# A mixture-of-experts encoder layer: who clears the gather buffers, unsized first gathers, pair sums in the last stage, and one guard around an unused position

## The chip, the cores and the metric

One core of one Trainium2 chip runs the whole layer in one launch. The metric is the device time of that core in microseconds; the profile adds one execution of the same program, with its span and every engine's instructions.

## The reference

One encoder layer over 1024 tokens of width 1024: a mixer (neighbourhood attention, a bidirectional RWKV-7 scan, pooling), then a hierarchical mixture of experts, each followed by a residual sum and a layer norm. The change touches the second half alone:

```python
u2 = layer_norm(x) * (1.0 + sc2) + sh2
# top-1 of 4 groups, then top-2 of its 8 experts; gate = pg_sel * softmax(top two logits)
hb = silu(u2[tok] @ w_gate[e]) * (u2[tok] @ w_up[e])      # 1024 -> 512
y[tok, j] = hb @ w_down[e]                                # 512 -> 1024, j = 0, 1
f = gate[:, 0] * y[:, 0] + gate[:, 1] * y[:, 1]
x = layer_norm(ALPHA * x + g2 * f) * ln2_gain + ln2_bias
```

All of it is in float32; a float32 matmul leaves two records of TensorE in the trace.

## The kernel before

After the mixer, `router` sorts the 2048 (token, choice) pairs into positions, each of one expert with up to 128, 64 or 32 rows. `route` builds on VectorE, GpSimd and ScalarE the table `idx` (which token's row goes to which partition of which position; 0 to 1023 is a row, anything above is skipped by the gather) and `code` (size and expert of each position, read by every engine as a register). Sixteen comparisons on GpSimd (L1267), each followed by a scaling on ScalarE (L1268), feed sixteen matmuls (L1323) whose result becomes `idx` (L1356). Meanwhile GpSimd clears the four row buffers `xg` with one memset (L1275), placed behind its last comparison. A barrier ends the router.

`experts` is written by hand, one program for each engine, with semaphores. There are 50 possible positions; the first 16 are always used, and from there each is under a condition on `code`. SyncE streams three 2 MB weight parts for each position through three buffers, waiting for the position's turn to be freed (the first three positions' weights are loaded before). GpSimd gathers the rows of the first four positions, later one more whenever a buffer is free; each gather reads the size of its position and picks one of three forms (32, 64 or 128 rows). `pipeline` gives the order on TensorE, ScalarE and VectorE: in step g, `head(g)` (gate and up products on TensorE, L1713 and L1721), `rows(g + 1)` (transposes of the next rows, L1692), `down(g - 1)` (L1747, L1758; on VectorE the scaling by g2 out of PSUM, L1781 and L1786), `turn(g)` (transposes of h, L1728). `by_size` is a nest of branches (L1512, L1514, L1516) around the code for 32, 128 and 64 rows; `if_used` (L1524) is one branch. On TensorE the step of the first unused position has nothing to do but `down` of the position before it: it passes over `head` by the branches of `by_size`, over `rows` and `turn` by one `if_used` each. GpSimd scatters each position's result rows to `ys_s` in DRAM, row 2 * token + j.

The last stage is written by `tail_plan` as three lists of operations. Eight 1 MB loads (L1595) bring `ys_s` back, tile tt with 128 tokens, token t on partition t with both choices beside each other. TensorE sums the two choices by two products with diagonal matrices of the gates `dg` (L1866), in two halves of 512 columns; tiles 2 and 5 also add ALPHA * x by a third product with `alpha`. For the other six VectorE adds ALPHA * x and takes the sum of the row out of PSUM (`sums`, L1878), for tiles 2 and 5 ScalarE does (L1875). Then, for each tile: VectorE the mean (L1883), ScalarE square with sum and root (L1895, L1897), VectorE two small operations (L1887, L1888), ScalarE the normalisation (L1901), VectorE gain and bias (L1891, L1892), SyncE the 512 KB store (L1639). The wait of an operation names the ones that it needs; each list runs in its order.

Of the kernel before, what the change touches and what calls it, by code (L numbers as in the profile page):

```python
# [13 lines left out]
OP = mybir.AluOpType  # L14
# [109 lines left out]
class Builder:  # L124
# [1082 lines left out]
    def route(self, p, ps):  # L1207
# [66 lines left out]
        with self.rtc.issue_after(last.ins):  # L1274
            nc.gpsimd.memset(self.xg, 0.0)  # L1275
# [185 lines left out]
    def experts(self):  # L1461
# [9 lines left out]

        gain, bias = self.late[:, 0], self.late[:, 1]
# [15 lines left out]
        names += [f"l{i}" for i in range(8)] + ["x1a", "x1b", "tail_pe", "tail_act", "tail_dve"]  # L1488
# [50 lines left out]
        def pipeline(e, rows, head, down, turn):  # L1539


            def step(g, old, c):
                new = size(e, g + 1) if g + 1 < NP else None
                head(g, c)
                if new is not None:
                    rows(g + 1, new)
                if g and down:
                    by_size(e, old, lambda t: down(g - 1, t))
                if turn:
                    turn(g, c)  # L1550
                if g + 1 == NP:
                    if down:
                        by_size(e, c, lambda t: down(g, t))
                elif down:
                    if_used(e, c, g, lambda: step(g + 1, c, new))
                else:
                    if_used(e, new, g + 1, lambda: step(g + 1, c, new))
# [9 lines left out]
        tail = self.tail_plan(sem, yall, x1a, of, ls, gain, bias, [(pgu[0], pgu[1]), tuple(pT), tuple(py)], junk)  # L1567
        with nc.Block() as blk:
            @blk.sync
            def _(e):  # L1570
# [9 lines left out]
                def finish(g):  # L1580
# [13 lines left out]
                    for tt in range(8):  # L1594
                        e.dma_start(yall[tt], self.ys_d[256 * tt:256 * tt + 256, :].rearrange("(t j) n -> t j n", j=2)  # L1595
# [39 lines left out]
                e.dma_start(g2, self.rows_d[3]).then_inc(sem("g2"), 16)  # L1635
                step(0, None)
# [6 lines left out]
            def _(e):  # L1643
# [38 lines left out]
            def _(e):  # L1682
# [41 lines left out]
                def turn(g, c):  # L1724
# [6 lines left out]
                    def both():  # L1731
                        e.wait_ge(sem("h"), g + 1)
                        with e.If(c > 1):
                            part((2, 3))
                        part((0, 1)).then_inc(sem("ht"), 1)
                    if_used(e, c, g, both)
# [96 lines left out]


# [8 lines left out]
    def tail_plan(self, sem, yall, x1a, of, ls, gain, bias, banks, junk):  # L1843
# [8 lines left out]
        dg, eps = self.late[:, 2:4].rearrange("p a (j n) -> p (a j) n", n=128), self.leps  # L1852
        gates = self.gtw.rearrange("p j t -> p (j t)")
        ident, alpha = self.C["ident"], self.C["alpha"]
# [3 lines left out]
        inside = lambda tt: tt in (2, 5)  # L1858
        pf = lambda tt: banks[tt % 3]

        def product(tt):
            def f(e):
                n = 3 if inside(tt) else 2
                for h in range(2):
                    for j in range(n):
                        i = e.matmul(pf(tt)[h], dg[:, tt + 8 * j] if j < 2 else alpha,  # L1866
                                     (yall[tt][:, j] if j < 2 else x1a[tt])[:, hs[h]], start=j == 0, stop=j == n - 1)
                return i
            free = [("sum1", tt - 3)] if tt > 2 else []
            op("pe", "mm", tt, [("dg0", tt), ("dg1", tt), (f"l{tt}", 16), ("x1" + "ab"[tt // 4], 16)] + free, f)  # L1870
# [38 lines left out]
        for tt in range(8):  # L1909
            product(tt)  # L1910
# [98 lines left out]
```

## Time and profile before

| | us |
|---|---|
| time, median of 3 runs | 1575.91 (1575.29 to 1577.81) |
| the profiled execution's own time | 1565.44 |
| its span, first to last instruction | 1563.6 |
| TensorE busy in the span | 1367.4 (87%) |
| VectorE busy | 778.7 (50%) |
| ScalarE busy | 571.8 (37%) |
| GpSimd busy | 380.4 (24%) |

The shares are averages over the mixer (to about 922 us), the router (to 947 us), the experts (to 1511 us) and the last stage, which have different limits. The profiled execution lies 10.47 us under the median of the timed runs; 1.84 us of its time lie around the span.

### The profile page before, as it was taken

To read this page: it belongs to the slowest core of one execution; us is meant where nothing else is said; L and a number is where in the kernel's file an instruction comes from. 1 tells how busy PE (TensorE), PEld (TensorE's weight loads), DVE (VectorE), ACT (ScalarE), POOL (GpSimd) and SP (SyncE) were. 2 spreads that over 40 slices of the span, in tenths; PEclk is the share of its full clock that TensorE was granted. 3 is DMA by queue.
4 is the path that set the end of the run, shared out by engine and by line. 5 is a ranking of instruction groups with operands and counts; after the bars stand their busy time and mean duration, and the time that the engine had idled before them with its cause. 6 is when DMAs were issued, how large, how long until landed. Compare 5 with 4: busy or idle time off the path is not lost. (4 is left out here: it accounts for less than half of the span.)

```text
span 1563.6 us, 24661 instructions
## 1 busy us (share of the span) xinstructions
PE 1367.4 (87%) x8190; PEld 923.9 (59%) x8190; DVE 778.7 (50%) x2002; ACT 571.8 (37%) x1182; POOL 380.4 (24%) x442
## 2 busy tenths in 40 slices
PE   5989999988869899999899745999999999899856
PEld 5778778766546677677788643444444444444422
DVE  6775886855883566565667972111111121211117
ACT  5663433414575667676544430000001000100006
POOL 3331232351337313700403331011101101111000
PEclk8999999996868899989999857999999999999968
DMA  9868899866422325315564475898878987998764
GB/s 259 223 200 303 284 318 327 298 211 186 145 64 69 93 72 150 88 35 150 187 262 162 167 275 208 338 351 324 330 291 341 380 324 306 362 369 349 262 248 193
DMA packets 163373, 371.49 MB, mean 238 GB/s; under 512 B 22880, under 2 KB 99009, under 8 KB 154227
## 3 DMA queue, kind: packets, MB, share of 16 engines
q1 hardware_dynamic: 155555, 350.59, 63.2%
q0 software_dynamic: 7632, 18.51, 3.7%
q8 instruction: 106, 1.74, 0.4%
q14 instruction: 80, 0.66, 0.1%
HBM read 365.47 MB, written 65.44 MB: 276 GB/s over the span
## 5 line engine op out<-in xcount | busy, mean ns | idle before, releaser
L1713 PE MATMUL m_pgu<-w,m_xT 128*128 128x512 f32 x448 | 197.0, 598 | 7.4 <-issue 7.2
L1713 PEld LDWEIGHTS m_pgu<-w,m_xT 128*128 128x128 f32 x448 | 84.7, 192 | 110.4 <-issue 110.3
L1656 POOL DMA_INDIRECT ys_s<-m_y,m_idx x37 | 35.0, 946 | 467.4 <-DVE m_y L1786 266.5
L197 PE MATMUL pg<-ul,w_h 128*128 128x512 f32 x320 | 128.2, 401 | 0.2 <-DVE ul L295 0.2
L196 PE MATMUL pg<-uh,w_h 128*128 128x512 f32 x320 | 126.7, 402 | 1.4 <-ACT uh L294 0.7
L198 PE MATMUL pg<-uh,w_l 128*128 128x512 f32 x320 | 126.8, 396 | 0.0
L1721 PE MATMUL m_pgu<-w,m_xT 128*32 128x256 f32 (+1 forms) x1312 | 108.0, 420 | 8.7 <-issue 8.3
L1747 PE MATMUL m_py<-w,m_hT 128*128 128x512 f32 x224 | 98.7, 594 | 9.6 <-issue 9.6
L1825 DVE TENSOR_TENSOR m_h<-m_sil,m_pgu 128x512 f32<-128x512 f32 x14 | 9.6, 688 | 192.4 <-PE m_pgu L1713 192.4
L1721 PEld LDWEIGHTS m_pgu<-w,m_xT 128*32 128x32 f32 (+1 forms) x1312 | 53.6, 116 | 54.5 <-issue 34.2
L210 DVE SCALAR_TENSOR_TENSOR acc<-wm,sc_c,acc 128x256 f32<-128x256 f32 x112 | 62.3, 557 | 27.8 <-DMA wm<-in_w_mod_dram 18.9
L1747 PEld LDWEIGHTS m_py<-w,m_hT 128*128 128x128 f32 x224 | 41.5, 190 | 57.1 <-issue 57.1
L1828 DVE TENSOR_TENSOR m_h<-m_sil,m_pgu 64x256 f32<-64x256 f32 (+1 forms) x23 | 10.8, 471 | 121.0 <-ACT m_sil L1796 121.0
L196 PEld LDWEIGHTS pg<-uh,w_h 128*128 128x128 f32 x320 | 60.6, 191 | 15.3 <-ACT uh L294 1.6
L197 PEld LDWEIGHTS pg<-ul,w_h 128*128 128x128 f32 x320 | 61.0, 191 | 14.1 <-issue 0.7
L198 PEld LDWEIGHTS pg<-uh,w_l 128*128 128x128 f32 x320 | 61.1, 191 | 13.3 <-issue 0.7
L945 DVE SCALAR_TENSOR_TENSOR sn<-s,fc,sf 64x64 f32<-64x64 f32 x168 | 47.5, 283 | 41.7 <-PE s L936 38.6
L756 PE MATMUL g<-zi,bk 64*128 64x128 f32 x384 | 54.2, 320 | 15.2 <-DMA bk<-bkd 9.3
L1758 PE MATMUL m_py<-w,m_hT 128*32 128x256 f32 (+1 forms) x656 | 56.6, 418 | 12.2 <-issue 12.2
L1781 DVE TENSOR_TENSOR m_y<-m_py,m_g 128x512 f32<-128x512 f32 x28 | 19.4, 692 | 88.0 <-PE m_py L1747 88.0
L756 PEld LDWEIGHTS g<-zi,bk 64*128 64x128 f32 x384 | 46.6, 219 | 28.0 <-issue 10.6
L1786 DVE TENSOR_TENSOR m_y<-m_py,m_g 32x256 f32<-32x256 f32 (+1 forms) x82 | 37.0, 451 | 52.3 <-PE m_py L1758 51.1
(523 smaller groups left out, 3017.8 us busy)
## 6 DMA issues: line engine op xcount, KB each, us to landing
w<-in_moe_w_gate_dram SPq DMA_DIRECT2D x37, 2048.0 KB, 8.4
w<-in_moe_w_up_dram SPq DMA_DIRECT2D x37, 2048.0 KB, 12.9
w<-in_moe_w_down_dram SPq DMA_DIRECT2D x37, 2048.0 KB, 15.9
wm<-in_w_mod_dram SPq DMA_DIRECT2D x128, 128.0 KB, 4.6
w<-in_w_in_dram SPq DMA_DIRECT2D x21, 512.0 KB, 6.7
hd<-h SPq DMA_DIRECT2D x18, 512.0 KB, 4.5
wm<-in_w_mod_dram SPq DMA_DIRECT2D x16, 512.0 KB, 6.3
w<-ys_s SPq DMA_DIRECT2D x8, 1024.0 KB, 13.0
```

The lines of the kernel that those rows point to most:

```text
L196: mm(out, lh[0], rh[0], start=start, stop=False)
L197: mm(out, lh[0], rh[1], start=False, stop=False)
L198: mm(out, lh[1], rh[0], start=False, stop=stop)
L210: nc.vector.scalar_tensor_tensor(acc, wm, self.sc_c[:, k:k + 1], acc, op0=OP.mult, op1=OP.add)
L756: nc.tensor.matmul(pa[h][:, j], bk[hs, j], zr[hs, j], start=True, stop=True)
L945: nc.vector.scalar_tensor_tensor(sn[H[h], H[h]], p[H[h], 2, H[h]], fc[H[h]], sf[H[h], H[h]], op0=OP.mult, op1=OP.add)
L1656: e.indirect_dma_start(out=self.ys_d, out_offset=off(idx[0:t, NP + g:NP + g + 1]), in_=y[0:t, g % NY], in_offset=None, bounds_check=2 * S ...
L1713: i = mm(pgu[q], xT[:, k], w[:, k], start=k == 0, stop=k == 7)
L1721: i = mm(pgu[0][o:o + t, 0:n], xT[:, k, 0:t], w[:, k, c:c + n], start=k == 0, stop=k == 7)
L1747: i = mm(py[nh], hT[:, 128 * f:128 * f + 128], wd[b][:, f, 512 * nh:512 * nh + 512], start=f == 0, stop=f == 3)
L1758: i = mm(py[0][o:o + t, 0:n], hT[:, 64 * j + t * a:64 * j + t * a + t], wd[b][:, f, c:c + n], start=f == 0, stop=f == 3)
L1786: i = e.tensor_mul(y[0:t, g % NY, c], py[0][t * j:t * j + t, 0:n], g2[0:t, c])
```

## The change

Five things change. (1) In `route` ScalarE clears `xg` (Copy of one constant column, broadcast, with scale 0), behind its own last scaling; GpSimd's memset goes. (2) In `experts` GpSimd's first four gathers take all 128 indices, without reading the size; the sizes are read after the fourth. (3) In the last stage each tile's `ys_s` rows are loaded so that a row and its pair lie on neighbouring partitions (two blocks of 128 rows); one product with a 128 x 64 matrix sums the pairs of a block (`pair` scaled by `rowg`, the gates in that order), and the two blocks fill partitions 0 to 63 and 64 to 127 of the bank. (4) There, tiles 0 to 6 get ALPHA * x by a product with `alpha` in front of (`residual`), and ScalarE takes them out of PSUM; VectorE keeps the sums of tile 7, and joins the normalisation and gain, and the root and bias, into two operations for each tile (`xm`, `add`), so that `rs`, `xn` and `gain` go. (5) In `pipeline`, for the engines that have `down` (TensorE and VectorE), one `if_used` stands around `head` and `rows`, and one around `turn` and the next step. Four small DMAs on SyncE's queue, behind that of `g2`, arrange `rowg`.

```diff
-            last = nc.gpsimd.tensor_scalar(ohr[:, j], C["iota128"], row[:, j:j + 1], None, op0=OP.is_equal)
-            nc.scalar.activation(ohs[:, j], ohr[:, j], AF.Copy, scale=C["orow1"][:, j:j + 1])
+            nc.gpsimd.tensor_scalar(ohr[:, j], C["iota128"], row[:, j:j + 1], None, op0=OP.is_equal)
+            last = nc.scalar.activation(ohs[:, j], ohr[:, j], AF.Copy, scale=C["orow1"][:, j:j + 1])
...
         with self.rtc.issue_after(last.ins):
-            nc.gpsimd.memset(self.xg, 0.0)
+            nc.scalar.activation(self.xg, C["iota128"][:, 0:1, None].to_broadcast([128, NX, D]), AF.Copy, scale=0.0)
...
             def step(g, old, c):
                 new = size(e, g + 1) if g + 1 < NP else None
-                head(g, c)
-                if new is not None:
-                    rows(g + 1, new)
-                if g and down:
-                    by_size(e, old, lambda t: down(g - 1, t))
-                if turn:
-                    turn(g, c)
...
+                def first():
+                    head(g, c)
+                    if new is not None:
+                        rows(g + 1, new)
+
+                def rest():
+                    if turn:
+                        turn(g, c)
...
+                else:
+                    if_used(e, c, g, first)
+                    if g:
+                        by_size(e, old, lambda t: down(g - 1, t))
+                    if_used(e, c, g, rest)
...
-                        e.dma_start(yall[tt], self.ys_d[256 * tt:256 * tt + 256, :].rearrange("(t j) n -> t j n", j=2)
+                        e.dma_start(yall[tt], self.ys_d[256 * tt:256 * tt + 256, :].rearrange("(s p) n -> p s n", s=2)
...
+                for s in range(2):
+                    for j in range(2):
+                        e.dma_start(rowg[j:128:2, s, :], self.gtw[64 * s:64 * s + 64, j, :]).then_inc(sem("rowg"), 16)
...
                 for g in range(NX):
+
+                    e.indirect_dma_start(
+                        out=xg[:, g], out_offset=None, in_=self.u2d, in_offset=off(idx[:, g:g + 1]),
+                        bounds_check=S - 1, oob_is_err=False).then_inc(sem(f"xg{g}"), 16)
+                for g in range(NX):
                     c.append(size(e, g))
-                    gather(g, c[g])
...
+                e.tensor_add(pair, ident[:, 0:128:2], ident[:, 1:128:2]).then_inc(sem("pair"), 1)
...
-        inside = lambda tt: tt in (2, 5)
+        inside = lambda tt: tt < 7
...
+        def residual(tt):
+            def f(e):
+                for h in range(2):
+                    i = e.matmul(pf(tt)[h], alpha, x1a[tt][:, hs[h]], start=True, stop=False)
+                return i
+            op("pe", "x1", tt, [("x1" + "ab"[tt // 4], 16)] + [(f"sum{h}", tt - 3) for h in range(2) if tt > 2], f)
...
+            def half(e, h):
+                for s in range(2):
+                    i = e.matmul(pf(tt)[h][64 * s:64 * s + 64, :], dg[:, 2 * tt + s], yall[tt][:, s, hs[h]],
+                                 start=not inside(tt), stop=True)
...
+        def centre(tt):
+            op("dve", "xm", tt, [("mean", tt), ("mm1", tt), ("late", 32)], lambda e: e.scalar_tensor_tensor(
+                xm(tt), of[tt], col(tt, 12), gain, op0=OP.add, op1=OP.mult))
+
+        def normal(tt):
             op("dve", "rec", tt, [("sd", tt)], lambda e: e.reciprocal(col(tt, 15), col(tt, 14)))
-            op("dve", "rs", tt, [("rec", tt)], lambda e: e.tensor_mul(col(tt, 16), col(tt, 12), col(tt, 15)))
...
+            op("dve", "add", tt, [("rec", tt), ("xm", tt), ("sq", tt)], lambda e: e.scalar_tensor_tensor(
+                of[tt], xm(tt), col(tt, 15), bias, op0=OP.mult, op1=OP.add))
...
-        def normal(tt):
-            op("act", "xn", tt, [("rs", tt)], lambda e: e.activation(of[tt], of[tt], AF.Identity, bias=col(tt, 16),
-                                                                    scale=col(tt, 15)))
...
+        for tt in range(2):
+            residual(tt)
         for tt in range(8):
+            if tt > 1 and inside(tt):
+                residual(tt)
             product(tt)
-        for tt in range(10):
-            if 0 < tt < 9:
-                rstd(tt - 1)
+        for tt in range(9):
             if tt < 8:
                 if not inside(tt):
                     sums(tt)
                 mean(tt)
-            if tt > 1:
-                affine(tt - 2)
-        for tt in range(9):
-            if tt < 8 and inside(tt):
-                sums(tt)
+                centre(tt)
             if tt:
                 normal(tt - 1)
-            if tt < 8:
-                deviation(tt)
+        for tt in range(8):
+            if inside(tt):
+                sums(tt)
+            deviation(tt)
```

## Rows read from the trace of the kernel before

**Rows 1.** The chain that ended last, end of experts and last stage: start, us, what.

```profile
1498.76 6.54 PE m_py L1758 x15
...
1510.88 5.23 DMA w<-ys_s
...
1516.35 6.32 PE m_pgu L1866 x8
...
1559.35 1.23 DVE w L1892
```

**Rows 2.** Busy time of the engines in stretches of 4 us, last stage.

```profile
1508.00:1512.00 4.00, 0.00 (x0) 0.00 (x0) 1.66 (x8) 0.00 (x0) 0.51 (x1) 0.50 0.39 76
...
1520.00:1524.00 4.00, 4.00 (x9) 1.76 (x8) 1.29 (x4) 0.00 (x0) 0.00 (x0) 0.79 1.01 424
...
1552.00:1556.00 4.00, 0.00 (x0) 0.00 (x0) 3.90 (x10) 2.65 (x5) 0.00 (x0) 0.55 0.33 131
```

**Rows 3.** Timeline of the router near 936 us: start, us, engine, line.

```profile
935.98 3.50 POOL L1275 MEMSET m_xg<- 128x4096 f32 x1
936.00 3.58 DVE L1312 TENSOR_SCALAR rt<-rt 128x16 int32<-128x16 int32 x1
936.06 0.40 ACT L1268 ACTIVATE rt<-rt,cst 128x128 fp32r<-128x128 f32 x1 [0.17 <-POOL rt L1267]
...
939.59 0.18 DVE L1342 TENSOR_SCALAR m_code<-m_code 1x50 int32<-1x50 int32 x1
...
946.66 0.19 DVE L1356 CAST m_idx<-rt 128x50 int32<-128x50 f32 x1
```

**Rows 4.** Groups of instructions by line and form, ScalarE and VectorE.

```profile
L1875 ACT ACTIVATE w<-m_py 128x512 f32<-128x512 f32 x4 | 2.3, 592 | 1.3 <-PE m_py L1866 1.3
...
L1895 ACT ACTIVATE w<-w,m_ls 128x1024 f32<-128x1024 f32 x8 | 9.2, 1146 | 25.9 <-DVE m_ls L1883 25.9
...
L417 DVE SCALAR_TENSOR_TENSOR t<-t,rows 128x1024 f32<-128x1024 f32 x6 | 7.3, 1218 | 0.0
...
L1878 DVE SCALAR_TENSOR_TENSOR w<-w,m_pgu 128x512 f32<-128x512 f32 x6 | 3.9, 684 | 12.8 <-PE m_pgu L1866 12.8
```

**Rows 5.** The chain that ended last, start of the experts.

```profile
947.63 0.52 POOLq L1499
...
948.53 0.04 POOLq L1648
...
949.40 2.44 DMA m_xg<-u_s,m_idx
```

**Rows 6.** Timeline: SyncE's first load of an expert's weights.

```profile
960.40 0.36 SPq L1577 DMA_DIRECT2D w<-in_moe_w_gate_dram  x1
```

**Rows 7.** DMA issues, start of the experts: KB each, median us to landing.

```profile
m_g<-rows_s SPq DMA_DIRECT2D x1, 512.0 KB, 3.4
```

**Rows 8.** Timeline, TensorE at full clock: 16 matmul records 64 and 128 wide.

```profile
1002.32 3.65 PE L1758 MATMUL m_py<-w,m_hT 128*64 128x512 f32 x16
...
1264.14 7.03 PE L1747 MATMUL m_py<-w,m_hT 128*128 128x512 f32 x16
```

**Rows 9.** Timeline of the last stage, one tile on ScalarE and VectorE.

```profile
1543.31 0.60 ACT L1875 ACTIVATE w<-m_py 128x512 f32<-128x512 f32 x1 [0.58 <-PE m_py L1866]
...
1544.61 0.21 DVE L1883 TENSOR_SCALAR m_ls<-m_ls 128x1 f32<-128x1 f32 x1 [0.82 <-ACT w L1875]
...
1545.60 1.14 ACT L1895 ACTIVATE w<-w,m_ls 128x1024 f32<-128x1024 f32 x1
...
1546.86 0.29 ACT L1897 ACTIVATE m_ls<-m_ls,m_le 128x1 f32<-128x1 f32 x1
```

**Rows 10.** TensorE's branches (PEldq), by line: ns min/median/max, first and last start.

```profile
L1512 PEldq COMPARE_BRANCH  x1: 440/440/440, 1491.3 to 1491.3; - x1
...
L1512 PEldq COMPARE_BRANCH  x1: 5522/5522/5522, 1492.4 to 1492.4; - x1
...
L1524 PEldq COMPARE_BRANCH  x67: 65/65/3813, 1179.0 to 1499.1; - x67
```

More of the change, by code (lines that the diff above doesn't have):

```diff
@@ L1470, in experts @@
         ls = sb("m_ls", [128, 8, 20])
+        pair = sb("m_pair", [128, 64])
+        rowg = sb("m_rowg", [128, 2, 8])
         gain, bias = self.late[:, 0], self.late[:, 1]
@@ L1487, in experts @@
         names = ["T0", "T1", "xT", "gu0", "gu1", "sil", "h", "h0", "ht", "hs", "y0", "y1", "e0", "e1", "late", "g2", "o"]
-        names += [f"l{i}" for i in range(8)] + ["x1a", "x1b", "tail_pe", "tail_act", "tail_dve"]
+        names += [f"l{i}" for i in range(8)] + ["x1a", "x1b", "pair", "rowg", "tail_pe", "tail_act", "tail_dve"]
         names += [f"{w}{b}" for w in "GUD" for b in range(NB)]
@@ L1543, in step @@
                 new = size(e, g + 1) if g + 1 < NP else None
-                head(g, c)
-                if new is not None:
-                    rows(g + 1, new)
-                if g and down:
-                    by_size(e, old, lambda t: down(g - 1, t))
-                if turn:
-                    turn(g, c)
[L1551 to L1555, printed above, removed]
-                else:
-                    if_used(e, new, g + 1, lambda: step(g + 1, c, new))
+                def first():
[5 more added lines that the diff above has]
+                        turn(g, c)
+                    if g + 1 == NP:
+                        if down:
+                            by_size(e, c, lambda t: down(g, t))
+                    elif down:
+                        step(g + 1, c, new)
+                    else:
+                        if_used(e, new, g + 1, lambda: step(g + 1, c, new))
+                if not down:
+                    first()
+                    rest()
+                else:
+                    if_used(e, c, g, first)
+                    if g:
+                        by_size(e, old, lambda t: down(g - 1, t))
+                    if_used(e, c, g, rest)
             c = size(e, 0)
@@ L1565, in wait @@
                 e.wait_ge(sem(name), v)
-        tail = self.tail_plan(sem, yall, x1a, of, ls, gain, bias, [(pgu[0], pgu[1]), tuple(pT), tuple(py)], junk)
+        tail = self.tail_plan(sem, yall, x1a, of, ls, gain, bias, pair, rowg, [(pgu[0], pgu[1]), tuple(pT), tuple(py)], junk)
         with nc.Block() as blk:
@@ L1729, in part @@
                         return i
[L1731 to L1736, printed above, removed]
+                    e.wait_ge(sem("h"), g + 1)
+                    with e.If(c > 1):
+                        part((2, 3))
+                    part((0, 1)).then_inc(sem("ht"), 1)
                 def down(g, t):
@@ L1840, in experts, with tail_plan @@
         ctx.close()
-    def tail_plan(self, sem, yall, x1a, of, ls, gain, bias, banks, junk):
+    def tail_plan(self, sem, yall, x1a, of, ls, gain, bias, pair, rowg, banks, junk):
         lists = {"pe": [], "act": [], "dve": []}
```

32 lines of the change are left out of this document (12 added, 20 removed).

## The prediction

> **What bounds the kernel now.** I read the page first, then the chain that ended last, then stretches of 4 us, and only then single rows; a share of the whole span says little, since each stage has its own limit. Three places of the chain are touched. In the router VectorE's chain of small operations builds `idx`, and nothing else can start before it. The experts are a long run of TensorE, started by the first gather and fed by weight loads whose first one waits for the first position; so what the start gains, the whole stage gains. The last stage starts when the loads of `ys_s` land: TensorE starts at 1516.35 and the last VectorE operation ends at 1560.58, 44.23 us later [rows 1]. In it two limits follow each other. At first TensorE is slow: the clock is 0.50 before it starts and 0.79 on average from 1520 to 1524, and its first eight records take 6.32 us [rows 1, 2]. Later VectorE is the limit: 3.90 of 4 us busy from 1552 to 1556, when TensorE has long finished [rows 2]. The loads are not: 8.4 MB at 424 GB/s leave one tile every 2.5 us [rows 2].
>
> **The change part by part.** The sum is made against the profiled execution's own 1565.44 us; the same microseconds are then taken from the median of 1575.91, since all of them lie in stages that both executions run.
>
> *Clearing the buffers.* GpSimd's memset runs from 935.98 for 3.50 us. VectorE's operation that starts at 936.00 takes 3.58 us, on 16 columns, and ends with the memset; the next one starts at 939.59 and takes 0.18 us [rows 3]. Without the memset that operation should end near 936.2, so `idx` is complete 3.4 us earlier, at 943.45 instead of 946.85. The clearing goes to ScalarE behind its last scaling, which ends at 936.46 [rows 3]. From 592 ns for 512 columns and 1146 ns for 1024 [rows 4] one column costs 1.08 ns, and 4096 of them 4.5 us: it ends at 941.0, 2.5 us ahead of the router's new end, which is its cover; nothing of ScalarE's is queued behind it in the router. At twice that length it would end at 945.5 and cost 2.1 us. Bounds of this part: 0 (if something else held VectorE) to 3.6; I take 3.4.
>
> *First gathers.* GpSimd begins to read the first size at 947.63 and reaches the first gather at 948.53; the gather starts at 949.40 and its rows are there 2.44 us after [rows 5]. Without the reading the 0.90 us go. Three things could take some of it back: the 512 KB load of `g2`, which is under way until 3.4 us after its issue [rows 7], four small DMAs queued behind it, and gathers of 128 indices in place of 32, whose surplus is skipped. If the rows come only after the load of `g2` (951.1) and four issues of 0.36 us behind it, they come 0.7 us later than the present 951.84. Bounds: -0.7 to 0.9; I take 0.6, since the rows follow the load of `g2` already now. The four DMAs also stand ahead of SyncE's weight loads, but the first of these is issued at 960.40 [rows 6], some 12 us after SyncE starts; the four need 1.5 us of them.
>
> Both gains move the first position, hence the first load and everything behind it.
>
> *The last stage.* Sixteen records of 64-wide products take 3.65 us, because two halves of the array work side by side; sixteen 128-wide ones take 7.03 [rows 8]. A tile's new product is eight 64-wide records, 1.83 us; its residual is four 128-wide ones, 1.76. The residuals of tiles 0 and 1 run right behind the last `down`, which ends at 1505.3 [rows 1], and are over before the loads land; but TensorE is then idle again for some 7 us, and I let it start slow, as before. Counting from its start at 0: full clock from 5.3 on (1521.65, between the stretch at 0.50 and the end of the one at 0.79 [rows 2]); up to there 2.65 us of full-clock work are done, and tiles 0 and 1, 3.65 of it, are ready at 6.3. Then five times 1.76 + 1.83 for tiles 2 to 6: 24.2. Tile 7, without a residual: 26.1.
>
> ScalarE for each tile: from its first sum at 1543.31 to the end of VectorE's mean at 1544.82 are 1.51 us, from the square at 1545.60 to the end of the root at 1547.15 are 1.55 [rows 9]: 3.1 with the gaps, under TensorE's 3.59. VectorE for each tile: mean 0.21, two operations on 1024 columns at 1.22 [rows 4, 9], the reciprocal and gaps 0.25: 2.9, under it too. So TensorE sets the pace, and the end is a tail on VectorE, in its order: sums of tile 6 on ScalarE and its mean at 25.3, `xm` of 6 at 26.5, `add` of 5 at 27.9, two sums of tile 7 at 0.68 [rows 4] to 29.2, mean 29.4, `xm` of 7 30.6, `add` of 6 32.0, `add` of 7 33.4. Against 44.23 that is 10.8 us less; the store behind it stays. If TensorE never ran slow, tile 7 would be ready at 23.4 and the gain 13.4; if the two halves did not work side by side, it would be ready at 39.5, and with the last sums, mean, `xm` and two `add` behind it the end lies at 45.3, a loss of 1.1. I take 10.8, because the 64-wide row has the same shape of work.
>
> The Trainium skill, "TensorE: Matmul & The Clock Gate", section "Measured speedup vs the span model", speaks against full overlap: three column tiles gave 2.38 times, not 3. If two gave 1.59 times, as an estimate from that page, a product would take 2.2 us and the gain would be 8 us. The row here has 7.03 / 3.65, 1.93 times.
>
> *The guard.* For the unused position TensorE passes three branches between 1491.3 and 1492.4, the first of 0.44 us, and then waits 5.52 us in a fourth, over the 32-row code of `down`; the last `down` starts at 1498.76 [rows 1, 10]. One guard in place of the three starts that long branch some 0.7 us earlier. Where it jumps on, the long wait stays: the same code is jumped over. Used positions keep their number of branches on TensorE (the guard of `turn` and that of the step become those of `first` and `rest`), and a guard that isn't taken costs 65 ns at the median of 67 [rows 10]; VectorE gets one more in each, in time that it waits for TensorE. Bounds: -3.8, the longest of the 67, if the longer jump brings a second long wait, to 5.5 if it brings none; I take 0.4, between nothing and the 0.7.
>
> The Trainium skill, "Runtime: NRT & Kernel Launch", section "Instruction fetch mechanics", says that a taken branch whose target lies outside the two pages at hand waits for a fetch of the target page. By it one longer jump may meet that wait just as four short ones did. It is the rule behind the first of the rivals below.
>
> The sum: 3.4 + 0.6 + 10.8 + 0.4 = 15.2 us. The profiled execution would take 1550.2, the median 1560.7.
>
> **The rivals.**
> - *The guard's jump waits twice.* Its target and the branch after it each wait, 3.8 us on top: 15.2 - 0.4 - 3.8 = 11.0, 1564.9. For it: the jump is longer than any of the three. Against it: over the code of `head` the present branch takes 0.44 us.
> - *The guard's jump doesn't wait.* The gap shrinks by 5.5: 15.2 - 0.4 + 5.5 = 20.3, 1555.6. Against it: the same code still separates the two places.
> - *The start gives nothing.* VectorE was held by something that ends with the memset by chance, and the gather waits for the load of `g2`: 15.2 - 4.0 = 11.2, 1564.7. Against it: two ends within 0.1 us of each other [rows 3].
> - *The change of the last stage doesn't do what it says.* The two 64-wide halves follow each other: 15.2 - 10.8 - 1.1 = 3.3, 1572.6. Against it: the 3.65 us.
> - *Slower.* The positions that are under a condition have their code in another order, and branches that were short wait for code. At 3.8 us for one [rows 10] four of them leave nothing of the gain, five make it slower, six give 1583.5. For it: such waits of several us exist in the trace. Against it: the number of branches and the code between them are the same.
>
> **How the numbers follow.** Chances: the forecast, within 4 us, 0.56; the guard waits twice 0.10; doesn't wait 0.10; the start gives nothing 0.06; the halves don't overlap 0.05; slower 0.06; several terms small together, so that it comes out within 0.2%, 0.04; sizes beyond 20 us 0.03. The range from 1554 to 1567 takes in the forecast and the three rivals around it, 0.82. A difference under 0.2%, 3.2 us, is about what a measurement of this kernel can't tell from none. Faster: 0.56 + 0.10 + 0.10 + 0.06 + 0.05 + 0.03 = 0.90; the same 0.04; slower 0.06.
>
> **What would show it.** Clearing: VectorE's operations near 936 take 0.2 us, ScalarE's Copy ends ahead of `idx`. Gathers: the first one starts 0.9 us earlier behind the barrier. Last stage: a product of eight records in 1.8 us at full clock, TensorE's last record 26 us after its first product, VectorE's last operation 33 us after it. Guard: one branch of several us ahead of the last `down`, as before. The prediction is wrong if the gap from the load of `ys_s` to the end shrinks by less than 7 us, or if the experts' stage between the first gather and the last `down` changes by more than 4.

## The result, and the profile after

| | before | after |
|---|---|---|
| time, median of 20 runs of each | 1575.78 us (1564.68 to 1584.72) | 1564.44 us (1555.95 to 1574.90) |
| ratio, with its 95% interval | | 0.9936 [0.9918, 0.9953] |
| the profiled execution's own time, its span | 1565.44, 1563.6 us | 1559.32, 1557.1 us |

The change makes the kernel 10.1 us faster (7.4 to 12.9), where 15.2 was forecast; the forecast of 1560.7 us lies 3.7 us under the median. The spans of the two profiled executions differ by 6.5 us alone. So the stages are read one by one.

**Router.** Timeline of the kernel after, near 937 us: start, us, engine and line, in brackets the idle time before it and what ended it.

```profile
937.38 0.15 DVE L1312 TENSOR_SCALAR rt<-rt 128x16 int32<-128x16 int32 x1
...
937.50 0.18 DVE L1342 TENSOR_SCALAR m_code<-m_code 1x50 int32<-1x50 int32 x1
...
937.74 3.60 ACT L1275 ACTIVATE m_xg<-cst 128x4096 f32<-128x4096 f32 x1
...
944.58 0.19 DVE L1356 CAST m_idx<-rt 128x50 int32<-128x50 f32 x1
```

These answer to [rows 3]. L1312, which took 3.58 us beside GpSimd's memset, takes 0.15; L1342 follows 0.12 us behind its start instead of 3.59. ScalarE clears in 3.60 us and is done at 941.34, 3.4 us ahead of `idx`. From the end of GpSimd's last comparison to the end of L1356 it was 10.82 us and is 7.37.

**Start of the experts.** The chain that ended last, kernel after:

```profile
946.39 2.68 DMA m_xg<-u_s,m_idx
949.06 0.67 issue
949.74 1.99 PE m_pT L1712 x8
```

and SyncE's two lines in the timeline there:

```profile
945.58 0.33 SPq L1648 DMA_DIRECT2D m_g<-rows_s  x1
...
945.95 2.42 SPq L1651 DMA_DIRECT2D m_rowg<-m_gt  x4
```

The load of `g2` is SyncE's first instruction behind the barrier. The gather starts 0.81 us behind it, where it was 1.74 (947.66 to 949.40). But TensorE takes its rows up 3.35 us after the gather's start, not 2.49 (0.67 of them lie behind the landing that the profile gives here; two more traces of this kernel have 3.17 and 3.52 us for the landing itself and 0.04 behind it). From the load of `g2` to TensorE it was 4.23 us and is 4.16: what the reading of the size cost is nearly all paid again, behind the gather's start.

**The unused position.** TensorE's branches by line, kernel after (ns min/median/max, start):

```profile
L1515 PEldq COMPARE_BRANCH  x1: 5748/5748/5748, 1497.0 to 1497.0; - x1
```

One long wait is left, as in [rows 10], 0.2 us longer. The guard in front of it takes 0.44 us (439 ns), and the long branch starts 2.74 us after the last gate and up product, where it was 3.40. From that product to the last `down`: 9.78 us before, 9.30 after.

**Last stage.** The chain, kernel after:

```profile
1514.64 5.35 DMA w<-ys_s
...
1520.12 3.68 PE m_pgu L1890 x8
1523.81 1.82 PE m_pT L1890 x8
1525.63 1.91 PE m_py L1883 x4
1527.55 1.87 PE m_py L1890 x8
...
1542.67 1.89 PE m_pgu L1890 x8
1544.59 0.70 ACT w L1900 x2
1545.63 1.28 DVE w L1915
...
1548.34 1.32 DVE w L1903 x4
...
1552.79 1.28 DVE w L1920
```

The stretches that answer to [rows 2] (busy us of PE, PEld, DVE, ACT, POOL with the number of instructions; PE's granted clock; DMA share; GB/s):

```profile
1520.00:1524.00 4.00, 3.88 (x10) 1.40 (x12) 0.00 (x0) 0.84 (x3) 0.00 (x0) 0.51 1.03 421
1552.00:1556.00 4.00, 0.00 (x0) 0.00 (x0) 2.04 (x3) 0.00 (x0) 0.00 (x0) 0.50 0.61 242
```

The first product (L1890, both halves of a tile) takes 3.68 us while the clock is granted at 0.51; from the second on a product takes 1.82 to 1.89 and a residual (L1883) 1.91. From 1523.81 to 1544.56 TensorE is the chain; behind ScalarE's sum of tile 6 it is VectorE, with `xm` and `add` of the last tiles and the two sums of tile 7. From the first product's start to the end of VectorE's last operation: 33.95 us (1520.12 to 1554.07), where it was 44.23 [rows 1].

**The experts between.** Busy time in the stretch from TensorE's first transpose to the last gate and up product, one row for each of four executions: the kernel before as shown,

```profile
951.89:1488.98 537.09, 500.74 (x3000) 249.54 (x3004) 89.49 (x177) 46.86 (x109) 67.24 (x70) 0.98 0.86 330
```

the kernel before in a second execution (below),

```profile
952.80:1500.15 547.35, 508.94 (x3000) 249.93 (x3004) 89.67 (x177) 46.96 (x109) 67.31 (x70) 0.97 0.84 324
```

the kernel after as shown,

```profile
949.74:1494.31 544.57, 506.56 (x3000) 248.64 (x3004) 89.41 (x177) 46.88 (x109) 66.73 (x70) 0.97 0.84 326
```

and the kernel after in a third execution (below).

```profile
946.52:1494.53 548.01, 506.25 (x3000) 248.46 (x3004) 89.78 (x177) 46.88 (x109) 66.47 (x70) 0.97 0.84 324
```

This stage is 537.1 us long in one execution of the kernel before and 547.4 in the other. Over the 14 traces of this study it goes from 537.1 to 553.2 us, and the time in it at the low clock (0.50, which is 1.2 of 2.4 GHz) from 16.8 us, in the shortest stage, to 40.4 and 45.1 us, in the two longest. The two go together: the stage is 0.53 us longer for each us at the low clock (a straight line through the 14 traces; correlation 0.90). Where some of that time comes from shows in the chain of the kernel after, at two of its gaps,

```profile
1115.72 2.17 issue
1117.89 5.24 PE m_py L1776 x16
...
1350.01 2.48 issue
1352.48 15.67 PE m_pgu L1733 x32
```

and in the stretches of these two pieces of work and of two pieces of the same lines elsewhere, without such a clock:

```profile
1117.89:1123.13 5.24, 5.24 (x17) 1.62 (x18) 0.00 (x0) 0.00 (x0) 0.00 (x0) 0.69 0.96 353
1227.57:1231.22 3.65, 3.65 (x17) 1.30 (x18) 0.00 (x0) 0.00 (x0) 0.00 (x0) 1.00 0.99 346
1352.48:1368.15 15.67, 15.67 (x34) 6.91 (x35) 0.00 (x0) 0.60 (x1) 1.60 (x2) 0.89 1.01 412
1391.89:1405.86 13.97, 13.97 (x34) 6.31 (x35) 0.00 (x0) 0.60 (x1) 1.82 (x2) 1.00 0.93 364
```

Twice TensorE issues nothing for over 2 us, and behind it the clock is granted at 0.69 and 0.89 on average and the work takes 1.6 and 1.7 us more than at 1.00. The profiled execution of before was a short one in this stage: 7.5 us shorter than that of after, whose router also ends its last comparison 1.4 us later. That is why the two spans differ by less than the medians.

### The profile page after: what moved, and what is told of

It reads as the page before. It is cut to its first block, busy times and chain, and to the rows that moved or that the text cites. A ratio compares the mean times of both kernels' runs of the same rounds, so it can differ in the third digit from the quotient of the medians.

```text
span 1557.1 us, 24710 instructions
## 1 busy us (share of the span) xinstructions
PE 1365.5 (88%) x8210; PEld 915.0 (59%) x8210; DVE 768.4 (49%) x1975; ACT 571.0 (37%) x1195; POOL 374.6 (24%) x441
## 3 DMA queue, kind: packets, MB, share of 16 engines
q8 instruction: 106, 1.74, 0.5%
## 5 line engine op out<-in xcount | busy, mean ns | idle before, releaser
L1765 PE MATMUL m_py<-w,m_hT 128*128 128x512 f32 x224 | 101.9, 608 | 9.9 <-issue 9.9
L1765 PEld LDWEIGHTS m_py<-w,m_hT 128*128 128x128 f32 x224 | 42.5, 195 | 59.6 <-issue 59.6
L1846 DVE TENSOR_TENSOR m_h<-m_sil,m_pgu 64x256 f32<-64x256 f32 (+1 forms) x23 | 10.8, 471 | 121.3 <-ACT m_sil L1814 114.7
L196 PEld LDWEIGHTS pg<-uh,w_h 128*128 128x128 f32 x320 | 60.2, 190 | 16.8 <-ACT uh L294 3.2
L756 PEld LDWEIGHTS g<-zi,bk 64*128 64x128 f32 x384 | 46.6, 219 | 28.5 <-issue 11.4
## 6 DMA issues: line engine op xcount, KB each, us to landing
w<-in_moe_w_down_dram SPq DMA_DIRECT2D x37, 2048.0 KB, 15.8
```

The lines of the kernel that those rows point to most:

```text
L196: mm(out, lh[0], rh[0], start=start, stop=False)
L756: nc.tensor.matmul(pa[h][:, j], bk[hs, j], zr[hs, j], start=True, stop=True)
L1765: i = mm(py[nh], hT[:, 128 * f:128 * f + 128], wd[b][:, f, 512 * nh:512 * nh + 512], start=f == 0, stop=f == 3)
```

## The experiments

Times beside a run are medians; a ratio is that to the kernel before on the same chip, in the same set of runs.

**Each part alone.** Four kernels, each the kernel before with one part. They share one set of 34 runs of the kernel before (1580.56 us).

*Clearing alone:*

```diff
-            nc.gpsimd.memset(self.xg, 0.0)
+            nc.scalar.activation(self.xg, C["iota128"][:, 0:1, None].to_broadcast([128, NX, D]), AF.Copy, scale=0.0)
```

> The kernel before with the clearing of the row buffers on ScalarE alone. Theory (GpSimd's memset holds VectorE's operations on 16 to 50 columns): those near 936 us take 0.15 to 0.35 us in place of 3.6 to 3.8; from the end of GpSimd's last comparison to the end of the last step of idx are 7.4 us in place of 10.8; the first transposes of the experts start 3.4 us earlier against that comparison, and the median falls by 3.4 us, unless what follows scatters by more. Rival (something else holds VectorE, and the memset only ends with it): VectorE's operations stay at 3.6 us, no gain.

1573.88 us, 0.9958 [0.9928, 0.9988]. Timeline of this kernel, VectorE and ScalarE near 938 us:

```profile
938.09 0.15 DVE L1312 TENSOR_SCALAR rt<-rt 128x16 int32<-128x16 int32 x1
...
938.46 3.60 ACT L1275 ACTIVATE m_xg<-cst 128x4096 f32<-128x4096 f32 x1
...
945.29 0.19 DVE L1356 CAST m_idx<-rt 128x50 int32<-128x50 f32 x1
```

Comparison to `idx` is 7.36 us, as with all parts. Taking the memset away is enough to make VectorE's operation short, so it was the memset that held it. The Trainium skill, "SBUF — State Buffer", section "Who interferes with whom", has a shared pair of ports between VectorE and GpSimd and none of ScalarE's: the trace agrees, 3.58 us beside the memset against 0.15 without it, and VectorE's longest operation there, L1320, takes 0.99 us beside ScalarE's Copy as it did behind the memset. The median falls by 6.6 us (1.9 to 11.4), which takes in the 3.4 of this stage.

*First gathers alone:*

```diff
+                    e.indirect_dma_start(
+                        out=xg[:, g], out_offset=None, in_=self.u2d, in_offset=off(idx[:, g:g + 1]),
+                        bounds_check=S - 1, oob_is_err=False).then_inc(sem(f"xg{g}"), 16)
+                for g in range(NX):
                     c.append(size(e, g))
-                    gather(g, c[g])
```

> The kernel before with the four unsized first gathers alone, without the small DMAs for the gates. Theory (the small DMAs behind the load of g2 take the gain back): the first gather starts 0.9 us earlier behind the barrier and its rows land 2.4 us after its start, so TensorE starts 0.9 us earlier. Rival (128 indices, or the load of g2, take longer to land): 3.0 to 3.4 us from start to landing, and TensorE starts at most 0.2 us earlier. The median moves by under 1 us in both, less than it can tell; the trace decides.

1577.14 us, 0.9985 [0.9963, 1.0007]. The chain of this kernel at the start of the experts:

```profile
952.54 2.99 DMA m_xg<-u_s,m_idx
```

The rows need 2.99 us, without any of the four small DMAs on SyncE's queue, and TensorE starts 3.84 us after the load of `g2`, some 0.4 earlier than with sizes. The landing is the rival's, TensorE's start lies between the two; the rival's two causes, 128 indices and the load of `g2`, are looked at further down.

*The last stage alone* (parts 3 and 4 with their four DMAs; the diff is that of `tail_plan` above):

> The kernel before with the changes of the last stage alone (pair sums, residuals ahead, ScalarE's sums, fused VectorE operations, with the small DMAs for the gates). Theory: from TensorE's first product to VectorE's last operation 34 us in place of 44.2, and the median 10.3 us lower. Rival (half of the 10 us is given back in the experts, because the small DMAs or the other addresses slow them): the last stage is as short, but the median falls by only 5 us.

1569.10 us, 0.9925 [0.9900, 0.9951]. The chain of this kernel, first and last links:

```profile
1529.25 3.49 PE m_pgu L1878 x8
...
1561.61 1.28 DVE w L1908
```

33.6 us from the first product to VectorE's last operation (1529.25 to 1562.89), where the whole change has 33.95; from the first issue of the loads of `ys_s` both have 39.43. The median falls by 11.9 us (7.7 to 15.8), so nothing like the rival's half is given back.

*The guard alone* (the diff is that of `pipeline` above):

> The kernel before with the guards of pipeline alone. Theory (one long branch remains ahead of the last down, and the rest of the experts scatters from run to run): TensorE's last down starts 9.3 us after its last gate and up products in place of 9.8, the median is within 2 us of the kernel before. Rival (the guards cost something in every conditional position): the experts' stage is 4 to 7 us longer, as in the one profile of the changed kernel, and the median with it.

1579.21 us, 0.9975 [0.9952, 0.9999]. TensorE's long branch in this kernel:

```profile
L1512 PEldq COMPARE_BRANCH  x1: 5875/5875/5875, 1510.3 to 1510.3; - x1
```

It starts 3.07 us after the last gate and up product, since the guard ahead of it took 0.72 us here, and the last `down` 9.75 us after, no earlier than before. In the nine traces with the guard this gap is 8.29 to 10.09 us, 9.39 in the mean; in the five without it 9.50 to 9.78, 9.65 in the mean. One long wait is there in all of them, 5.30 to 5.52 us without the guard and 5.66 to 5.90 in eight with it (4.75 in the ninth): what the guard saves ahead of it, the branch partly takes back. The experts' stage is 544.9 us here, the median of the five traces without the guard 544.8: the rival's longer stage is not borne out.

**The small DMAs late.** The change, with the four DMAs for `rowg` moved from the start to SyncE's loads of `ys_s`:

```diff
+                    for s in range(2):
+                        for j in range(2):
+                            e.dma_start(rowg[j:128:2, s, :], self.gtw[64 * s:64 * s + 64, j, :]).then_inc(sem("rowg"), 16)
                     wait(e, "T1", g + 1)
...
                 e.dma_start(g2, self.rows_d[3]).then_inc(sem("g2"), 16)
-                for s in range(2):
-                    for j in range(2):
-                        e.dma_start(rowg[j:128:2, s, :], self.gtw[64 * s:64 * s + 64, j, :]).then_inc(sem("rowg"), 16)
```

> The changed kernel with the four small DMAs for the gates moved from the start of SyncE's program to its end, ahead of the loads of the last stage. Theory (they and the 128 indices share the loss of the first gather): from SyncE's first DMA behind the barrier to TensorE's first transposes 3.8 us in place of 4.2, as with the gathers alone; the last stage as in the changed kernel. Rival (the run alone with the gathers was quicker by chance): 4.1 to 4.2 us again.

1563.93 us, 0.9928 [0.9906, 0.9951]. The chain at the start of its experts:

```profile
943.32 3.04 DMA m_xg<-u_s,m_idx
946.36 0.04 issue
946.41 1.99 PE m_pT L1712 x8
```

From the load of `g2` to TensorE: 3.90 us. Without the small DMAs there the traces have 3.84, 3.90, 4.24 and 3.90 (first gathers alone, this one, and the two of the combined version below); with them 4.16, 4.03, 4.37, 4.14 and 3.86; with sized gathers 4.22 to 4.38. The theory that the four DMAs take the gain falls, but for perhaps 0.1 us. What is common to all nine is the gather without a size: from its start to TensorE's first transpose 3.0 to 3.6 us, where the five with sizes have 2.5 to 2.65.

The number of indices is not enough to explain that. The second gather has 128 indices too. DMA issues, the second gather alone, median us to landing: a second trace of the changed kernel, then of the kernel before:

```profile
m_xg<-u_s,m_idx POOLq DMA_INDIRECT x1, 2.3
```

```profile
m_xg<-u_s,m_idx POOLq DMA_INDIRECT x1, 2.2
```

Over the eight traces that show it the second unsized gather lands 2.25 to 2.49 us after its start, the sized one, in the one trace that shows it, 2.23. It starts 2.26 us after the issue of the load of `g2`, the first one 0.81. That load lands 3.2 to 3.45 us after its issue, sized gathers or not. In all 11 traces that show this landing, TensorE starts 0.6 to 1.2 us behind it, whether the gather started 1.74 or 0.81 us after the load's issue. So the rows look as if they waited for that load; no run moved the load, so this is not shown.

The last stage was expected as in the changed kernel, and is not: from the first issue of the loads to VectorE's last operation it is 40.20 us, where the changed kernel has 39.43. The second product is slow here as well (the clock is granted at 0.53 from 1524 to 1528), so a last stage with the same instructions can differ by 0.8 us:

```profile
1526.05 2.65 PE m_pT L1890 x8
```

**TensorE kept busy before the first product.** The residuals of tiles 0 and 1 are computed three times (the last one counts):

```diff
-        def residual(tt):
+        def residual(tt, warm=False):
...
-                    i = e.matmul(pf(tt)[h], alpha, x1a[tt][:, hs[h]], start=True, stop=False)
+                    i = e.matmul(pf(tt)[h], alpha, x1a[tt][:, hs[h]], start=True, stop=warm)
...
+        for _ in range(2):
+            for tt in range(2):
+                residual(tt, True)
```

> The changed kernel with the two first residuals computed three times over, so that TensorE works until the loads of ys land; the result is the same. Theory (the slow clock at the start of the last stage costs 2.7 us): the first product of eight records takes 1.9 us in place of 3.7, from it to VectorE's last operation are 31.3 to 32 us in place of 34. Rival (another limit stands right behind, ScalarE's first tile with its table load or the landing of the loads): under 1 us of gain.

1562.10 us, 0.9922 [0.9900, 0.9944]. Timeline of this kernel at the start of the last stage:

```profile
1518.53 1.88 PE L1883 MATMUL m_pT<-w,cst 128*128 128x512 f32 x4
...
1521.07 1.94 PE L1890 MATMUL m_pgu<-w,m_xg 128*64 128x512 f32 x8 [0.66 <-DMA w<-ys_s]
...
1523.62 1.94 PE L1890 MATMUL m_pT<-w,m_xg 128*64 128x512 f32 x8 [0.62 <-DMA w<-ys_s]
```

TensorE computes up to 1520.4, and the first product takes 1.94 us instead of 3.68. But the second one has to wait 0.62 us for its load, and of the 1.74 us 0.9 are left at the end: 38.50 us from the first issue of the loads of `ys_s` to VectorE's last operation, against 39.43 (39.43 and 39.44 in two more traces of the changed kernel). That is the rival's "under 1 us".

**The sums back on VectorE.** The change, with ScalarE taking tiles 2 and 5 out of PSUM alone, and residuals for these two only:

```diff
-        inside = lambda tt: tt < 7
+        inside = lambda tt: tt in (2, 5)
...
-        for tt in range(2):
-            residual(tt)
         for tt in range(8):
-            if tt > 1 and inside(tt):
+            if inside(tt):
                 residual(tt)
```

> The changed kernel with the sums of tiles 0, 1, 3, 4, 6 and 7 on VectorE again and residuals for tiles 2 and 5 alone, as before; pair sums and fused operations stay. Theory (before, VectorE set the pace of the last stage with 4.1 us for each tile): TensorE is done early, VectorE needs 2.9 + 1.4 us for each of the six tiles, and from TensorE's first product to VectorE's last operation are 38 to 40 us, between 44.2 of before and 34.0 of the changed kernel. Rival (the pair sums alone bring the gain, because TensorE was the limit): 34 us again, or less, since TensorE has five products fewer.

One execution: 1559.95 us. Timeline and chain of this kernel: VectorE's first sum, then the last tile's work.

```profile
1522.25 0.69 DVE L1903 SCALAR_TENSOR_TENSOR w<-w,m_pgu 128x512 f32<-128x512 f32 x1 [8.75 <-PE m_pgu L1890]
```

```profile
1520.24 3.68 PE m_pgu L1890 x8
...
1549.43 1.23 DVE w L1903 x4
...
1553.79 1.28 DVE w L1920
```

34.83 us from the first product to the end (1520.24 to 1555.07), only 0.9 more than with the sums on ScalarE. The theory's 38 to 40 falls. So moving the sums and adding the residuals on top of the rest is worth some 0.9 of the 10.3 us, by one execution, where a last stage with the same instructions differs by 0.8. What is left gives the rest: the first sum starts 2.0 us after the first product's start, where it was 6.4 (the timeline of the kernel before has it here,

```profile
1522.71 0.69 DVE L1878 SCALAR_TENSOR_TENSOR w<-w,m_pgu 128x512 f32<-128x512 f32 x1 [12.76 <-PE m_pgu L1866]
...
1551.58 0.68 DVE L1878 SCALAR_TENSOR_TENSOR w<-w,m_pT 128x512 f32<-128x512 f32 x1
```

since its two sums waited for one signal behind a product twice as long; in the change each half of a product has its own, `mm0` and `mm1`, which the description of the change doesn't name); and from the start of the last tile's first sum to the end it is 5.7 us (from 1549.35 in the timeline), where it was 9.0 (1551.58 to 1560.58). These are 4.4 and 3.3 of the 9.4 us, the remaining 1.8 lie between. The first sum tells a little too much: the first tile's mean, behind its second sum, comes 3.2 us earlier (4.5 us after the first product's start, where it was 7.7). Pair sums, signals by half and joined operations were not run apart.

**The edits that seemed to help, together.** The small DMAs late, the residuals three times, tile 3's sums on VectorE, and `add` of the tile before ahead of `mean` up to tile 6:

```diff
-        inside = lambda tt: tt < 7
+        inside = lambda tt: tt not in (3, 7)
...
-        for tt in range(9):
-            if tt < 8:
-                if not inside(tt):
-                    sums(tt)
-                mean(tt)
-                centre(tt)
-            if tt:
+        for tt in range(8):
+            if 0 < tt < 7:
                 normal(tt - 1)
+            if not inside(tt):
+                sums(tt)
+            mean(tt)
+            centre(tt)
+        normal(6)
+        normal(7)
```

> The changed kernel with the four small DMAs late, the residuals of tiles 0 and 1 computed three times over, the sums of tile 3 on VectorE, and the root and bias of each tile up to 5 ahead of the mean of the next. Theory (TensorE's pace, then VectorE's queue behind its last product, set the last stage): TensorE's last product ends 1.9 us earlier by the missing residual and 0.9 by the clock, and the tail behind it is 1.6 shorter: from the first of the loads of ys to VectorE's last operation 35 us in place of 39.4, and the first gather 0.2 us earlier. Rival (VectorE or ScalarE becomes the limit at once): 37 us or more. The median should be 15 us or more under the kernel before by the theory, 12 by the rival.

1562.24 us against 1579.95, 0.9895 [0.9856, 0.9933]. Timeline of this kernel, ScalarE and VectorE in the middle of the last stage:

```profile
1543.00 1.15 ACT L1924 ACTIVATE w<-w,m_ls 128x1024 f32<-128x1024 f32 x1 [0.53 <-DVE m_ls L1908]
...
1544.60 0.17 DVE L1919 RECIPROCAL m_ls<-m_ls 128x1 f32<-128x1 f32 x1 [0.32 <-ACT m_ls L1926]
...
1546.25 1.15 ACT L1924 ACTIVATE w<-w,m_ls 128x1024 f32<-128x1024 f32 x1 [0.53 <-DVE m_ls L1908]
```

From the first issue of the loads to VectorE's last operation it is 38.07 us (37.64 in a second trace), 1.4 less than the 39.43 of the changed kernel. A tile takes 3.25 us (1543.00 to 1546.25), ScalarE waits 0.53 of them for VectorE's mean and VectorE 0.32 for ScalarE's root: with less for TensorE to do, the two wait for each other in turn. So the stage follows the rival (37 us or more), and the time, 16.6 us less, the theory's 15 or more; the second set below decides what that time is worth.

**The kernel before once more,** one execution beside the others:

> The kernel before once more, for a second profile. Theory (its first profile had little slow clock by chance): the experts' stage from the first transposes to the last gate and up products takes 540 to 550 us in place of 537, with more time at the slow clock. Rival (the kernel before is always at 537 and the changed ones are slower there): 537 us again.

1574.25 us, span 1572.4. Its row of the experts stands above: the stage alone is 10.3 us longer than in the first profile of the same kernel.

**The change twice more, and the combined version beside it.**

> The changed kernel once more, for a second profile and its times beside those of the kernel before on the same chip. Theory (the parts add up, and the experts' stage scatters by chance with the time at the slow clock): the last stage 34 us, idx 7.4 us behind the last comparison, the experts' stage anywhere from 537 to 553 us, longer by about half the additional time at the slow clock, and a median 11 to 14 us under the kernel before. Rival (the change makes the experts' stage longer): 544 us or more again, and 8 us or less.

1564.66 against 1575.57 us, 0.9927 [0.9902, 0.9953]: 11.5 us less, as the theory has it. The experts' stage is 547.9 us with 34.5 at the low clock, within the theory's range and over the rival's 544 too; the rival's 8 us or less is not borne out.

> The changed kernel again, beside a set of runs of the kernel before of its own. Theory A (the traced stages give the whole gain, 14.4 us; the smaller timed differences were scatter of the rest): ratio near 0.991, 0.989 to 0.993. Rival B (something outside these stages, in the experts' stage, gives 3 to 4 us back whenever all parts are together): ratio 0.993 to 0.995 again, and an experts' stage over 546 us. The trace should show the same fixed stages: end of the last comparison to idx 7.36, last stage 42.4 to 42.5 from the first issue of the loads of ys_s to the last VectorE operation.

1566.84 against 1573.29 us, 0.9936 [0.9908, 0.9964], and 548.0 us in the experts' stage: the ratio and the stage that the second theory expected, though one trace of the kernel before has 547.4 us there as well. (The 42.4 to 42.5 us of the expectation count 3.0 us behind VectorE's last operation; without them they are the 39.4 above.)

> The version with the small loads late, residuals of tiles 0 and 1 three times, tile 3's sums on VectorE and normal(tt - 1) ahead of mean(tt), next to the changed kernel on the same chip. Theory A (its last stage is 1.4 us shorter and nothing else differs): 0.1% below the changed kernel's ratio, less than the intervals can tell. Rival B (the whole difference of the earlier ratios, 0.9895 against 0.9927 to 0.9936, is real): 0.3 to 0.4% below it.

1568.49 against the same 1573.29 us, 0.9957 [0.9933, 0.9981]. The second theory falls: the combined version is not 0.3% below the changed kernel. The first, whose 0.1% is less than the intervals, is neither borne out nor ruled out. The 0.9895 did not come again, on another chip; the two ratios of this version average to 0.9926, the three of the changed kernel to 0.9933. Its last stage is shorter in both traces, but no time shows that it beats the changed kernel.

## Why the prediction was right, and where its sizes were off

The sign, the order of the parts and the range held. By its steps, from the traces (the mean of two executions of the kernel before and three of the changed one, where not said otherwise):

- *Clearing:* forecast 3.4, measured 3.45. VectorE is free at once, ScalarE's clearing ends well ahead of `idx`. Its length was overestimated (4.5, measured 3.60), which costs nothing. That something else held VectorE is ruled out by the kernel with this part alone.
- *First gathers:* forecast 0.6, measured 0.1 (4.30 to 4.19 us from the load of `g2` to TensorE). The start moved by 0.93 as forecast. The step that failed is the choice of 0.6 "since the rows follow the load of `g2` already now": that premise speaks for no gain, since an earlier start doesn't move that load. From the start of the first gather without a size to TensorE it is 3.0 to 3.6 us, where it was 2.5 to 2.65. Both the load and the 128 indices were named as things that could take the gain back, and sized as if they did not. The second gather, with 128 indices too but started 2.26 us after the issue of that load, lands in 2.25 to 2.49 us, so the indices alone are not the cause; the load of `g2` fits the traces and was not tested. The four small DMAs, named beside them, are not what does it.
- *Last stage:* forecast 10.8, measured 10.3 in the first pair of profiles and 10.0 between the means (43.87 and 33.88 us from the first product on). The two halves do work side by side: eight 64-wide records in 1.82 to 1.89 us, forecast 1.83. Tile 7 is ready 26.14 us after the first product, forecast 26.1; VectorE ends at 33.95, forecast 33.4, since its 1024-column operations take 1.28 us and not 1.22. The slow first product was forecast too. That tile 7 is ready on the forecast's tenth is luck: TensorE was slow for 3.7 us and not 5.3, so tiles 0 and 1 were ready at 5.5 instead of 6.3 us, and a residual with its product took 3.78 us instead of 3.59, five times over, which takes the 0.8 us back. And it is not TensorE's new pace alone that gives the gain: with the old division of the sums it was 9.4 in one execution.
- *Guard:* forecast 0.4, measured 0.5 in the first pair of profiles and 0.3 as the mean of all traces with and without it; one long wait remains in each. With single gaps up to 1.8 us apart, the runs don't tell this term from nothing. The Trainium skill, "Runtime: NRT & Kernel Launch", section "Instruction fetch mechanics", has a taken branch outside the pages at hand wait for a fetch; the trace agrees in that the wait is still there, here for 4.75 to 5.90 us, and in that in each of the 14 traces one packet of 16 KB of the queue that the profile calls instruction (q8) moves within it, in the first one at 1495.18 for 1.36 us.
- *The rivals:* two long waits, none, halves that follow each other, a start that gives nothing: none of them is in the traces. Against the slower one stand the experts' stages: 537.1 to 553.2 us in five traces with the old order of branches (mean 545.2), 541.1 to 551.2 in nine with the new one (mean 546.0), with 31.3 and 31.5 us at the low clock in the mean.

Without the experts' stage and what lies ahead of GpSimd's last comparison, the span holds 90.5 and 88.3 us in the two executions before, 75.2, 74.7 and 75.2 in the three after: 14.4 us less, near the forecast sum of 15.2. That the median lies in the range is in part luck: the interval of the difference, 7.4 to 12.9 us, leaves out both 15.2 and 14.4, and the room above the forecast was made for rivals that didn't happen. The times give 10.1, 11.5 and 10.1 (1 minus each ratio, times the median before). The 3 to 4 us between must lie in the experts' stage or ahead of the router's last comparison, which together go from 1473 to 1498 us over the 14 traces; one trace of an execution can't show a shift of 3 us in that. Whether an earlier start makes the experts' stage that much longer, or the mixer differs, stays open.

Open is also why the four parts alone add up to 24.8 us by their times (0.42, 0.15, 0.75 and 0.25% of 1580.56). Each lies 0.1 to 0.25% above what its stage shows; their intervals, 0.22 to 0.30% to either side, make at least 8 us for the sum (an estimate that takes them as independent), and they share their runs of the kernel before. Chance in that one median is not the only way to read it: a second set of the kernel before on the same chip, beside the combined version, has 1579.95, where two other chips have 1575.57 and 1573.29. The 0.9895 of the combined version came on that chip too. The kernel before may run slower there than the changed ones do; the changed kernel itself was not run on that chip, so this was not shown.

One test that the prediction set for itself was too narrow: it would count as wrong if the stage from the first gather to the last `down` changed by more than 4 us. In the first pair it grew by 7.9 (549.36 to 557.22), and the same kernel before, run twice, differs by 10.3 (549.36 and 559.64).

## What to carry to other kernels

Before two traces are compared, trace the same kernel twice: here a stage of 540 us that was hardly edited varied by 10 us between executions, as much as the whole change was worth, and even a last stage with the same instructions by 0.8. Where two engines' operations end together, take one of them away and look whether the other gets short; it was the cheapest gain here. When a stage is limited by a chain of tiles, look first at what its first and last tile wait for: an earlier first sum and a shorter queue behind the last tile gave most of the 10 us, and the shift of work between the engines some 0.9. And when an earlier start of a transfer is to gain time, ask first what its data come behind: the first gather started 0.93 us earlier, and its rows came 0.1 us earlier.

## What the runs showed of the hardware that was not expected

- From the start of the first unsized gather, of 128 indices, to TensorE it is 3.0 to 3.6 us; with sizes it is 2.5 to 2.65. The second unsized gather, started 2.26 us after the issue of the load of `g2`, lands 2.25 to 2.49 us after its start, as fast as the sized one (2.23).
- ScalarE's Copy of a broadcast column into 4096 columns takes 3.60 us, 0.88 ns each, where 512 and 1024 columns out of PSUM and SBUF had given the estimate of 1.08 from [rows 4].
- SyncE needs 7.39 us to issue the eight loads of `ys_s` with a row and its pair on neighbouring partitions, where it needed 4.20, and 2.42 us for four DMAs of a few KB; the first of the loads isn't late by it.
- A gap of over 2 us in TensorE's work can cost nearly as much again behind it: 1.6 and 1.7 us in the two shown, with a granted clock of 0.69 and 0.89. The two longest gaps of that stage in the same trace, 2.83 and 3.77 us, cost 2.9 and 2.7 us more behind them (10.02 us for 7.11 and 9.80 for 7.09, the clock at 0.61 and 0.64 there). Behind three other gaps of 2.2 to 2.4 us the work took its usual time.
